# Weight rings of a retention and dilated mixer: four units of hi and lo over two raw slots

## The chip, the core and the metric

The kernel runs on one core of a Trainium2 chip. The metric is the device time of one launch in microseconds (us): the median of several runs. A profiled execution gives the trace, with a span from the first to the last instruction.

## What is computed

Two decoder layers over 512 tokens of width 1024. Each layer adds half of a SwiGLU network, then a token mixer, then half of another SwiGLU network, each on the RMS-normed input. The mixer of layer 0, which the change is about, is

```
h = rms_norm(x, norm_g);  proj = h @ w_in          # 1024 -> 3584
rq, rk, rv, rg, dq, dk, dv = split(proj)           # 8 heads of 64 each
ret = group_norm(retention(rotary(rq), rotary(rk), rv)) * silu(rg)
dil = dilated_attention(rotary(dq), rotary(dk), dv)
out = concat([ret, dil]) @ w_out
```

Layer 1 has a stick-breaking attention in its place. Inputs, weights and output are float32.

## The kernel before

**Two parts of every number.** A float32 operand is cut into `hi` (rounded to the type float32r that TensorE multiplies) and `lo`, the rest; `mm3` gives three matmuls for one product: hi by hi, hi by lo, lo by hi.

**Units.** Weights come in units of 128 x 1024 float32 (512 KB); one unit is a projection of 128 output columns (24 matmuls of 512 columns in `proj_steps`), or half of four heads' values. For every unit a raw copy is loaded by SP's queue into a slot of the role `wraw`, and hi and lo go into two slots of the role `whl`. `give` says which slots a role goes around, and `B` takes the next; a slot is free again when its last reader is done. Ten slots are for weights: before the change four are raw and six hold hi and lo, so three units of hi and lo.

**Two ways to make lo.** `weight` (`split`) casts hi on ScalarE (ACT) and subtracts on VectorE (DVE). In the mixer `weight_dma` is used for g, rq, rk, rv, dq, dk and dv (27 units go this way, since the first of the four gate units goes by `weight`): ACT casts hi, ACT writes minus hi into lo, and GpSimd (POOL) issues a DMA that adds the float32 weight from memory to what lies in lo. DVE has no part in it.

**Order of the mixer.** Four gate units are projected into PSUM banks of the tag `acc` (three of them), the norm's factor `r` comes from one matmul after the first, and `token_r` transposes it on TensorE. Then `stream` goes over the units: rq and rk of the first head pair, the two units of rv for four heads (`values`, two passes of 8 steps, of six matmuls of 256 columns each; both units are read in both passes), rq and rk of the next pair, and so on. `flow.run(n)` runs n steps of it; between them stand the attention's own matmuls: scores (`begin`), and `attend`. On TensorE (PE) this order is fixed by `ordered`. After a projection, DVE turns it (`rot_steps`) with a table that is loaded for each pair (`rot_q`, `rot_k`, 512 KB each), and `pack_q` and `pack_k` move the parts of q (tile `sp`) and of k (tile `ah`) into their places (`qk`, `qlo`) by small DMAs on SP's queue; the scores wait for these. DMA waits stand in SP's queue in order too.

**Output projections.** `out_ffn` computes eight tiles of 128 output columns from 22 chunks in three pieces (8, 7 and 7 chunks, a unit each). Between the pieces units of layer 1's mixer are split ahead (`cut_ahead`): loaded, split, and hi and lo stored to memory. The first four entries of the list are instead the units of rv, which `centre` prepares and stores (`centred`). The last argument of `out_ffn` says how many entries of the list are done there; over tiles 0 to 6 they are spread as evenly as whole numbers allow, tile 7 has none.

Of the kernel before, what the change touches and what calls it, by code (L numbers as in the profile page):

```python
# [18 lines left out]
ALU = mybir.AluOpType  # L19
# [16 lines left out]
def trunk(ctx: ExitStack, tc: tile.TileContext, a: dict, out: bass.AP):  # L36
# [20 lines left out]
    def oldest(role):  # L57

        n = turn_of[role] % len(roles[role])
        return roles[role][n:] + roles[role][:n]  # L60
# [31 lines left out]
    def f32(ap):  # L92
        return ap.bitcast(F32)
# [94 lines left out]

    BY_DMA = ["hyb_" + n for n in ("g", "rq", "rk", "rv", "dq", "dk", "dv")]

    def weight_dma(src, cols):
        raw = B((P, 1024), F32, "wraw")
        hi, lo = (B((P, 1024), F32R, "whl")[:, :cols] for _ in range(2))
        nc.sync.dma_start(raw[:, :cols], src)
        nc.scalar.copy(out=hi, in_=raw[:, :cols])
        nc.scalar.mul(out=lo, in_=f32(hi), mul=-1.0)
        nc.gpsimd.dma_start(lo, src, accum_op=ALU.add)
        return hi, lo

    turns = [0]  # L200
# [85 lines left out]
    def norm_r(ss, epsr=None):  # L286
        while pending:
            norm_sum(*pending.pop(0))
        ps = PS("po")
        mm(ps, ones_ms, ss, start=True, stop=True)  # L290
        r = rstd(ps, NORM_EPS, eps_n, "r")
        if epsr is not None:
            nc.vector.tensor_scalar(out=epsr, in0=ps, scalar1=NORM_EPS, scalar2=GN_EPS, op0=ALU.add, op1=ALU.mult)
        return r
# [288 lines left out]
    def mixer_roles():  # L583
        o = others()
        give(qk=o[:4], v=o[4:8], sp=o[8:11], ah=o[11:14], misc=o[14:15], qlo=o[15:17])
        give(**{f"o{i}": o[17 + i:18 + i] for i in range(8)})
        qlo[:] = [B((P, 2, SEQ), F32R, "qlo") for _ in range(2)]
        for l in qlo:
            nc.gpsimd.memset(f32(l[H1, :, :]), 0.0)
# [241 lines left out]
    def hybrid(ss, gcol_next):  # L831
        order["on"] = True
        mixer_roles()
        gates, held = [], []
        for p in range(4):
            held.append(ACC())
            if p == 0:
                w = weight(a["hyb_g"][0], D)
                proj_tile(None, held[-1], w)
            else:  # L840
                proj_tile(("hyb_g", p), held[-1])
            if p == 0:
                epsr = hpool.tile([P, SEQ], F32, tag="ss", name=nm("epsr"))
                r = norm_r(ss, epsr)
                continue
            if p == 1:
                rtm = token_r(r)
                rtm2 = cpool.tile([P, NB], F32, tag="rtm2", name="rtm2")
                nc.vector.tensor_mul(out=rtm2, in0=rtm, in1=rtm)
                act_set(SILU)  # L850
            for ps in held:
                g = T()
                nc.vector.tensor_mul(out=g, in0=ps, in1=r)
                if len(gates) % 2 == 0:
                    gg = B((P, 2, SEQ), F32, f"o{6 + len(gates) // 2}")
                gates.append(gg[:, len(gates) % 2, :])
                func(gates[-1], g, AF.Silu)
            held = []
        bd = const("bd", P)
        act_set(LNEXP)  # L860
        rot_d = table(a["rot_dil"], "misc")
        for i in range(2):
            nc.gpsimd.tensor_tensor(out=rot_d[:, i, :], in0=rot_d[:, i, :], in1=r, op=ALU.mult)
        outs, vs = [], [[] for _ in range(4)]
        q, k = [], []

        def qk(i):
            if i < 4:
                yield from rot_steps(("hyb_rq", i), table(a["rot_q"][i], "o4"), sw_r, lambda y: pack_q(y, "sp"), q)
                yield from rot_steps(("hyb_rk", i), table(a["rot_k"][i], "o5"), sw_r, lambda y: pack_k(y, "ah"), k)  # L870
            else:
                yield from rot_steps(("hyb_dq", i - 4), rot_d, sw_d, lambda y: pack_q(y, "sp", -0.125), q)
                yield from rot_steps(("hyb_dk", i - 4), rot_d, sw_d, lambda y: pack_k(y, "ah"), k)

        def stream():
            yield from qk(0)
            yield from values(("hyb_rv", 0), rtm2, vs[0])
            for i in range(1, 8):
                yield from qk(i)
                if i in (2, 4, 6):  # L880
                    yield from values(("hyb_rv" if i == 2 else "hyb_dv", (i // 2) % 2), rtm2 if i == 2 else rtm, vs[i // 2])
            yield from out_first("hyb_oa", outs)

        flow = Flow(stream())
        flow.run(26)
        dmask = None
        ready, o = {}, None

        def begin(h):

            nonlocal dmask
            p, e = h // 2, h % 2
            flow.until(k, p + 1)
            if h < 8:
                with tc.high_priority(offset=2 * SOON):
                    ready[h] = ret_scores(e, q[p], k[p], ("ah", "sp")[h % 2])
            else:
                if h == 8:
                    dmask = T(tag="r2")
                    nc.sync.dma_start(dmask, a["dmask"])  # L900
                with tc.high_priority(offset=2 * SOON):
                    ready[h] = dil_scores(e, q[p], k[p], dmask)

        begin(0)
        flow.run(27)
        for h in range(16):
            p, e = h // 2, h % 2
            if h >= 8:
                with tc.high_priority(offset=2 * SOON):
                    ready[h] = dil_turn(e, ready[h], ("ah", "sp")[h % 2])  # L910
                flow.run(2)
            if h < 15:
                begin(h + 1)
            flow.run(5)
            flow.until(vs[p // 2], NB)
            if e == 0:
                o = T(tag="oo")
            attend(vs[p // 2], p, e, ready.pop(h), o)
            if e == 0:
                flow.run(7 if h < 8 else 5)  # L920
            elif h < 8:
                ret_norm(p, o, gates[p], bd, epsr, outs, flow, 6)
            else:
                out_pair(o, outs)
                flow.run(4)
        for _ in flow.steps:
            pass
        ss = out_second("hyb_ob", outs, gcol_next)
        order["on"] = False
        return ss  # L930
# [162 lines left out]
    ahead = [lambda k=("hyb_rv", g, u): centre(k) for g in range(2) for u in range(2)]  # L1093
    ahead += [lambda u=u: cut_ahead(*u) for u in sb]
    us = ffn_seven(sums, a["wd0"], a["wq0"], 0, first)
    ss = out_ffn(a["f1_out"][0], us, 8, ahead, 16)
    ss = hybrid(ss, 16)
    us = ffn_seven(lambda: norm_r(ss), a["wd1"], a["wq1"], 16)
    ss = out_ffn(a["f2_out"][0], us, 24, ahead, 12)
    us = ffn_seven(lambda: norm_r(ss), a["wd2"], a["wq2"], 24)  # L1100
    ss = out_ffn(a["f1_out"][1], us, 32, ahead, 12)
    ss = stick(ss, 40)
    us = ffn_seven(lambda: norm_r(ss), a["wd3"], a["wq3"], 40)
    out_last(a["f2_out"][1], us, 48)
# [126 lines left out]
```

## Time and profile before

| | |
|---|---|
| median of 3 runs | 1932.62 us (1932.16 to 1934.15) |
| the profiled execution's own time | 1934.09 us |
| its span | 1932.4 us |
| PE busy | 1910.3 us (99%) |
| ACT, DVE, POOL busy | 1059.0, 1304.9, 165.8 us |
| mean granted TensorE clock | 0.997 |
| moved by DMA | 341 MB, 176 GB/s over the span |

Busy time of PE is that of overlapping matmuls, whose ends are modelled. The stages that matter here lie, in us from the span's start, at about 270 to 357 (first output projection), 357 to 391 (gates and first rq, rk), 391 to 413 (first values and first scores), 413 to 605 (the rest of the mixer), 605 to 620 (second output projection of the mixer).

### The profile page before, as it was taken

What the parts mean: (1) busy time and instruction counts of PE and PEld (TensorE: products, weight loads), DVE (VectorE), ACT (ScalarE), POOL (GpSimd) and SP (SyncE); (2) the same over time, 40 slices, a digit from 0 to 9 for tenths busy, and PEclk for the clock granted to TensorE, in tenths of its full rate; (3) what the DMA queues carried; (4) which work ended last, traced back from release to release, by engine and by line L of the source; (5) the groups of instructions that cost most, each with busy time, mean ns of one, the idle gap of its engine ahead of it and who ended that gap; (6) DMA issues with size and microseconds to landing.
All of it is one profiled execution on the core that took longest, in us unless ns stands there. A gap on an engine that the chain in (4) does not pass through costs nothing.

```text
span 1932.4 us, 29858 instructions
## 1 busy us (share of the span) xinstructions
PE 1910.3 (99%) x11648; PEld 1716.8 (89%) x11648; DVE 1304.9 (68%) x1854; ACT 1059.0 (55%) x1506; POOL 165.8 (9%) x285
## 2 busy tenths in 40 slices
PE   9999999989999999999999999999999999999998
PEld 7999988778888899998889999888888888999887
DVE  8767855346777877674477677443888878777534
ACT  6466734545776456663344567332666644666423
POOL 0011000112100001100000110000222200111000
PEclk9999999999999999999999999999999999999999
DMA  6386689889852457767734775667555443767433
GB/s 228 101 202 167 140 277 338 249 225 237 178 131 84 140 140 180 167 192 254 276 131 110 197 170 148 208 225 232 161 185 152 137 137 104 201 164 163 117 92 121
DMA packets 107837, 341.00 MB, mean 176 GB/s; under 512 B 13232, under 2 KB 14896, under 8 KB 107696
## 3 DMA queue, kind: packets, MB, share of 16 engines
q1 hardware_dynamic: 90992, 278.54, 44.0%
q0 software_dynamic: 16560, 60.30, 18.0%
q8 instruction: 91, 1.49, 0.3%
q14 instruction: 50, 0.41, 0.1%
q10 hardware_dynamic: 144, 0.26, 0.0%
HBM read 280.33 MB, written 37.75 MB: 165 GB/s over the span
## 4 chain that ended last, share of the span: by engine, by line
PE 94%; DMA 3%; DVE 2%; issue 1%; ACT 1%; SPq 0%; POOL 0%; DVEq 0%; ACTq 0%; POOLq 0%
PE acc L126 46%; PE att L126 45%; PE po L126 2%; DVE whl L225 1%; DMA whl<-centred 1%; PE att L129 0%; DMA cut_sb_k<-whl 0%; DMA qk<-ah 0%; DMA qk<-sp 0%; DVE h L256 0%; DMA cut_sb_v<-whl 0%; DMA wraw<-f_out 0%; ACT whl L224 0%; DMA x<-xT 0%; DMA cut_sb_q<-whl 0%
## 5 line engine op out<-in xcount | busy, mean ns | idle before, releaser
L224 ACT CAST whl<-wraw 128x1024 fp32r<-128x1024 f32 (+4 forms) x308 | 302.8, 989 | 459.0 <-PE acc L126 199.9
L225 DVE TENSOR_TENSOR whl<-wraw,whl 128x1024 fp32r<-128x1024 f32 (+4 forms) x308 | 352.2, 1147 | 259.2 <-ACT whl L224 232.2
L126 PE MATMUL acc<-u,whl 128*128 128x512 f32 (+1 forms) x2244 | 483.5, 377 | 2.1 <-DVE whl L225 2.1
L126 PEld LDWEIGHTS acc<-u,whl 128*128 128x128 f32 x2244 | 403.3, 188 | 80.8 <-DVE whl L225 3.7
L126 PE MATMUL att<-fT,whl 128*128 128x256 f32 x3072 | 379.1, 283 | 0.0
L126 PEld LDWEIGHTS att<-fT,whl 128*128 128x128 f32 x3072 | 373.5, 192 | 0.3
L126 PE MATMUL acc<-h,whl 128*128 128x512 f32 x1248 | 302.1, 394 | 0.9 <-DVE whl L225 0.6
L126 PE MATMUL att<-fB,whl 128*128 128x256 f32 x2304 | 287.2, 283 | 0.0
L126 PEld LDWEIGHTS att<-fB,whl 128*128 128x128 f32 x2304 | 281.2, 192 | 0.2 <-DMA whl<-wq 0.2
L126 PEld LDWEIGHTS acc<-h,whl 128*128 128x128 f32 x1248 | 232.8, 188 | 53.1 <-issue 2.9
L452 POOL DMA_DIRECT2D whl<-wq x88 | 76.4, 868 | 1022.4 <-ACT whl L451 763.0
L450 ACT CAST whl<-wraw 128x1024 fp32r<-128x1024 f32 x88 | 92.4, 1050 | 83.8 <-PE att L126 83.8
L126 PE MATMUL att<-h,whl 128*128 128x512 f32 x576 | 135.8, 389 | 0.0
L126 PEld LDWEIGHTS att<-h,whl 128*128 128x128 f32 x576 | 108.4, 188 | 22.6
L451 ACT ACTIVATE whl<-whl 128x1024 fp32r<-128x1024 f32 x88 | 93.3, 1060 | 2.7
L225 DVE TENSOR_TENSOR whl<-p,whl 128x1024 fp32r<-128x1024 f32 x32 | 39.2, 1224 | 69.5 <-ACT whl L224 69.5
L126 PE MATMUL acc<-whl,h 128*128 128x256 f32 x576 | 75.9, 287 | 4.3 <-DMA whl<-centred 4.3
L126 PEld LDWEIGHTS acc<-whl,h 128*128 128x128 f32 x576 | 73.4, 194 | 5.8 <-DMA whl<-centred 4.7
L323 DVE SCALAR_TENSOR_TENSOR x<-acc,x 128x512 f32<-128x512 f32 (+1 forms) x34 | 22.4, 658 | 69.5 <-PE acc L126 69.4
L225 DVE TENSOR_TENSOR u<-uq,u 128x512 fp32r<-128x512 f32 x88 | 58.9, 688 | 13.4 <-ACT u L224 12.8
L936 POOL TENSOR_SCALAR_AFFINE_SELECT t<-t 128x128 f32<-128x128 f32 x128 | 46.2, 383 | 190.0 <-DVE t L953 124.4
L224 ACT CAST u<-uq 128x512 fp32r<-128x512 f32 x88 | 52.6, 617 | 17.3 <-PE att L126 10.3
(184 smaller groups left out, 2171.8 us busy)
## 6 DMA issues: line engine op xcount, KB each, us to landing
wraw<-wq SPq DMA_DIRECT2D x128, 512.0 KB, 5.0
whl<-wq POOLq DMA_DIRECT2D x88, 512.0 KB, 6.9
wraw<-f_out SPq DMA_DIRECT2D x68, 448.0 KB, 4.3
wraw<-wd SPq DMA_DIRECT2D x46, 512.0 KB, 3.7
wraw<-f_out SPq DMA_DIRECT2D x34, 512.0 KB, 4.7
cut_sb_q<-whl SPq DMA_DIRECT2D x16, 512.0 KB, 3.8
cut_sb_k<-whl SPq DMA_DIRECT2D x16, 512.0 KB, 3.5
cut_sb_v<-whl SPq DMA_DIRECT2D x16, 512.0 KB, 4.8
```

The lines of the kernel that those rows point to most:

```text
L126: return ordered(nc.tensor.matmul(*args, **kw))
L224: nc.scalar.copy(out=hi, in_=src)
L225: nc.vector.tensor_tensor(out=lo, in0=src, in1=f32(hi), op=ALU.subtract)
L323: nc.vector.scalar_tensor_tensor(out=x[d][:, sl], in0=ps[:, sl], scalar=0.5, in1=x[d][:, sl], op0=ALU.mult, op1=ALU.add)
L450: nc.scalar.copy(out=hi, in_=raw)
L451: nc.scalar.mul(out=lo, in_=f32(hi), mul=-1.0)
L452: nc.gpsimd.dma_start(lo, src, accum_op=ALU.add)
L936: nc.gpsimd.affine_select(out=t[:, at:at + P], in_=t[:, at:at + P], pattern=[[1, P]], compare_op=ALU.is_gt, fill=0.0, base=0, channel_mult ...
```

## The change

In the mixer of layer 0 the ten weight slots are dealt out anew: two raw slots and four units of hi and lo, and back to four and three before the last part of its output projection. In `weight_dma` minus hi is taken from the raw unit (rounded as it is written) and comes in the program ahead of hi, with its DMA. The first gate products come after the third gate projection instead of the second, `token_r` with them. The first scores come six steps of the stream later. Of the 40 entries split ahead, 14, 13 and 13 are done in the three output projections in place of 16, 12 and 12.

```diff
+    def minus_hi(lo, src, raw):
+
+        nc.scalar.mul(out=lo, in_=raw, mul=-1.0)
+        nc.gpsimd.dma_start(lo, src, accum_op=ALU.add)
+
     def weight_dma(src, cols):
         raw = B((P, 1024), F32, "wraw")
         hi, lo = (B((P, 1024), F32R, "whl")[:, :cols] for _ in range(2))
         nc.sync.dma_start(raw[:, :cols], src)
+        minus_hi(lo, src, raw[:, :cols])
         nc.scalar.copy(out=hi, in_=raw[:, :cols])
-        nc.scalar.mul(out=lo, in_=f32(hi), mul=-1.0)
-        nc.gpsimd.dma_start(lo, src, accum_op=ALU.add)
         return hi, lo
...
         mixer_roles()
+        raws, ring = oldest("wraw"), oldest("whl")
+        give(wraw=raws[2:], whl=ring + raws[:2])
         gates, held = [], []
         for p in range(4):
...
                 r = norm_r(ss, epsr)
+            if p < 2:
                 continue
-            if p == 1:
+            if p == 2:
                 rtm = token_r(r)
...
         flow = Flow(stream())
-        flow.run(26)
+        flow.run(32)
...
         begin(0)
-        flow.run(27)
+        flow.run(21)
...
         for _ in flow.steps:
             pass
+        raws, ring = oldest("wraw"), oldest("whl")
+        give(wraw=raws + ring[:2], whl=ring[2:])
         ss = out_second("hyb_ob", outs, gcol_next)
...
-    ss = out_ffn(a["f1_out"][0], us, 8, ahead, 16)
+    ss = out_ffn(a["f1_out"][0], us, 8, ahead, 14)
...
-    ss = out_ffn(a["f2_out"][0], us, 24, ahead, 12)
+    ss = out_ffn(a["f2_out"][0], us, 24, ahead, 13)
...
-    ss = out_ffn(a["f1_out"][1], us, 32, ahead, 12)
+    ss = out_ffn(a["f1_out"][1], us, 32, ahead, 13)
```

The order of instructions is set by a scheduler from the program's order and its own estimates, so three places of it are shown. The last number of a name only tells tiles apart.

First, TensorE around the first scores (`att` tiles from `qk` and `qlo`; `acc` from `whl` and `h` are the second pass of the first values). Before, they come after the second of its eight steps:

```order
L126 MATMUL acc_3811<-whl_3745,h_2804 128x256 x2
L126 MATMUL acc_3811<-whl_3746,h_2804 128x256
L126 MATMUL acc_3811<-whl_3745,h_2804 128x256
L126 MATMUL att_3824<-qk_3688,qk_3738 128x384
L126 MATMUL att_3824<-qlo_3458,qk_3738 128x384
```

In the changed kernel, after the eighth:

```order
L126 MATMUL acc_3793<-whl_3758,h_3437 128x256 x2
L126 MATMUL acc_3793<-whl_3759,h_3437 128x256
L126 MATMUL acc_3793<-whl_3758,h_3437 128x256
L126 MATMUL att_3842<-qk_3670,qk_3720 128x384
L126 MATMUL att_3842<-qlo_3440,qk_3720 128x384
```

Nothing else moves on TensorE here: the six steps that stood behind the scores now stand ahead of them.

Second, SP's queue around the moves of the first q and k, which these scores wait for (`sp` is q's, `ah` is k's; `o<-rot_q` and `o<-rot_k` are the tables of the second pair, `wraw` the raw units). Before:

```order
L194 DMA wraw_3990<-hyb_rq 128x1024
L194 DMA wraw_4064<-hyb_rk 128x1024
L734 DMA o_576_3889<-rot_q 128x1024
L654 DMA qk_3688<-sp_3685 64x512 x2
L654 DMA qlo_3458<-sp_3685 64x512
L654 DMA qk_3688<-sp_3685 64x512 x2
L654 DMA qlo_3458<-sp_3685 64x512
L734 DMA o_585_3939<-rot_k 128x1024
L654 DMA qk_3738<-ah_3735 64x512 x4
L194 DMA wraw_4123<-centred_0_2767 128x1024
```

In the changed kernel:

```order
L199 DMA wraw_3972<-hyb_rq 128x1024
L658 DMA qk_3670<-sp_3667 64x512 x2
L658 DMA qlo_3440<-sp_3667 64x512
L658 DMA qk_3670<-sp_3667 64x512 x2
L658 DMA qlo_3440<-sp_3667 64x512
L738 DMA o_570_3871<-rot_q 128x1024
L658 DMA qk_3720<-ah_3717 64x512 x4
L738 DMA o_579_3921<-rot_k 128x1024
L199 DMA wraw_4046<-hyb_rk 128x1024
L199 DMA wraw_4105<-centred_0_2767 128x1024
```

One table moved from ahead of q's moves to behind them, the other, with a raw unit, from ahead of k's moves to behind them.

Third, ACT ahead of the first values (before, `whl_3745` and `whl_3746` are hi and minus hi of rv's first unit, `whl_3776` and `whl_3777` of its second; `o` are the gates). Before:

```order
L195 CAST whl_3745<-wraw_3744 128x1024
L108 ACTIVATE o_535_3601<-t_3635 128x512
L102 ACT_TABLE_LOAD
L196 ACTIVATE whl_3746<-whl_3745 128x1024
L195 CAST whl_3776<-wraw_3775 128x1024
L196 ACTIVATE whl_3777<-whl_3776 128x1024
```

In the changed kernel (`whl_3727` and `whl_3728` are the first unit's, `whl_3758` and `whl_3759` the second's):

```order
L201 CAST whl_3727<-wraw_3726 128x1024
L193 ACTIVATE whl_3728<-wraw_3726 128x1024
L108 ACTIVATE o_529_3583<-t_3581 128x512
L201 CAST whl_3758<-wraw_3757 128x1024
L193 ACTIVATE whl_3759<-wraw_3757 128x1024
L108 ACTIVATE o_529_3583<-t_3617 128x512
L102 ACT_TABLE_LOAD
```

Both units of rv now stand ahead of the last gate and the table load, a unit earlier than before. The scheduler still puts hi first in these two.

## Rows read from the trace of the kernel before

**Rows 1.** The page's part 1, busy time of each engine: us, share of the span, instructions.

```profile
PE 1910.3 (99%) x11648; PEld 1716.8 (89%) x11648; DVE 1304.9 (68%) x1854; ACT 1059.0 (55%) x1506; POOL 165.8 (9%) x285
```

**Rows 2.** The waits of PE over the whole span: who waited for whom, us in total, times, longest.

```profile
PE acc L126 <- DMA whl<-centred: 4.3, 2, 3.2
PE att L126 <- DMA qk<-ah: 3.0, 1, 3.0
PE acc L126 <- DVE whl L225: 2.7, 3, 1.5
```

**Rows 3.** The timeline of PE from the end of the first output projection on: start, us, instructions, and in brackets the idle time before with what ended it.

```profile
342.71 14.84 PE L126 MATMUL acc<-u,whl 128*128 128x512 f32 x64 [1.46 <-DVE whl L225]
...
369.53 22.02 PE L126 MATMUL acc<-h,whl 128*128 128x512 f32 x96
391.39 3.15 PE L126 MATMUL acc<-whl,h 128*128 128x256 f32 x25
397.71 4.46 PE L126 MATMUL acc<-whl,h 128*128 128x256 f32 x35 [3.16 <-DMA whl<-centred]
405.21 0.42 PE L126 MATMUL att<-qk,qk 128*128 128x384 f32 x1 [3.05 <-DMA qk<-ah]
...
406.84 5.70 PE L126 MATMUL acc<-whl,h 128*128 128x256 f32 x36
...
426.80 0.33 PE L126 MATMUL att<-qk,qk 128*128 128x384 f32 x1
...
428.08 3.57 PE L126 MATMUL acc<-h,whl 128*128 128x512 f32 x15
...
442.40 1.58 PE L126 MATMUL acc<-whl,h 128*128 128x256 f32 x11 [1.11 <-DMA whl<-centred]
...
445.04 4.53 PE L126 MATMUL acc<-whl,h 128*128 128x256 f32 x36
```

**Rows 4.** Stretches of time: length, busy us of PE, PEld, DVE, ACT and POOL with their instructions, granted clock, busy share of the DMA engines, GB/s.

```profile
370.00:375.00 5.00, 5.00 (x24) 4.13 (x23) 1.50 (x3) 2.20 (x4) 2.41 (x3) 1.00 0.67 155
375.00:380.00 5.00, 5.00 (x24) 4.14 (x23) 0.69 (x1) 2.53 (x3) 0.87 (x1) 1.00 0.89 205
380.00:385.00 5.00, 5.00 (x23) 4.14 (x23) 0.69 (x1) 3.93 (x4) 0.20 (x1) 1.00 0.80 196
385.00:390.00 5.00, 5.00 (x23) 4.14 (x23) 3.10 (x6) 2.75 (x3) 1.52 (x2) 1.00 0.78 140
395.00:400.00 5.00, 2.29 (x19) 2.29 (x20) 0.63 (x1) 0.00 (x0) 0.00 (x0) 1.00 1.07 256
400.00:405.00 5.00, 2.17 (x19) 1.96 (x17) 0.97 (x2) 0.95 (x2) 0.00 (x0) 1.00 1.04 295
405.00:410.00 5.00, 4.79 (x25) 4.62 (x26) 1.72 (x3) 1.81 (x4) 1.48 (x4) 0.66 0.13 40
407.00:408.00 1.00, 1.00 (x7) 1.00 (x6) 0.96 (x3) 0.59 (x1) 0.60 (x2) 0.50 0.00 0
```

**Rows 5.** The timeline of POOL: the DMAs that add the weight to the second unit of rv, of the first and of the second four heads' values.

```profile
388.56 0.86 POOL L197 DMA_DIRECT2D whl<-centred  x1 [2.90 <-ACT whl L196]
...
432.61 0.88 POOL L197 DMA_DIRECT2D whl<-centred  x1 [2.22 <-ACT whl L196]
```

**Rows 6.** The timeline of ACT ahead of the first values. L195 is hi, L196 minus hi; the first pair is that of rv's first unit, the second that of its second.

```profile
380.49 1.05 ACT L195 CAST whl<-wraw 128x1024 fp32r<-128x1024 f32 x1 [2.91 <-PE acc L126]
381.45 0.62 ACT L108 ACTIVATE o<-t 128x512 f32<-128x512 f32 x1
382.09 1.28 ACT L102 ACT_TABLE_LOAD   x1
383.38 1.06 ACT L196 ACTIVATE whl<-whl 128x1024 fp32r<-128x1024 f32 x1
385.93 1.05 ACT L195 CAST whl<-wraw 128x1024 fp32r<-128x1024 f32 x1 [1.48 <-PE acc L126]
387.01 1.06 ACT L196 ACTIVATE whl<-whl 128x1024 fp32r<-128x1024 f32 x1
```

**Rows 7.** DMA issues of single stretches, with the size and the us from issue to landing, in this order: a raw unit of rv at 360 to 380, rv's first unit at 383 to 388, its second at 388 to 389, a table and the later second unit at 432 to 434.

```profile
wraw<-centred SPq DMA_DIRECT2D x1, 512.0 KB, 5.1
whl<-centred POOLq DMA_DIRECT2D x1, 512.0 KB, 5.4
whl<-centred POOLq DMA_DIRECT2D x1, 512.0 KB, 9.1
o<-rot_q SPq DMA_DIRECT2D x1, 512.0 KB, 11.6
whl<-centred POOLq DMA_DIRECT2D x1, 512.0 KB, 9.7
```

**Rows 8.** The chain of work that ended last, in order of time: start, us, what.

```profile
396.14 8.25 DMA qk<-ah
```

**Rows 9.** The timeline of ACT, and then of PE, at the end of the second output projection, whose tile 6 has two entries split ahead.

```profile
956.32 1.79 ACT L224 CAST whl<-wraw 128x896 fp32r<-128x896 f32 x2 [6.19 <-DMA cut_sb_k<-whl]
...
960.58 9.36 PE L126 MATMUL acc<-u,whl 128*128 128x512 f32 x40 [0.65 <-DVE whl L225]
```

**Rows 10.** The timeline of ACT (the logarithm of the norm's factor) and of DVE (the first two gate products).

```profile
364.85 0.67 ACT L108 ACTIVATE t<-po,eps_n 128x512 f32<-128x512 f32 x1
...
368.86 1.29 DVE L853 TENSOR_TENSOR t<-acc,r 128x512 f32<-128x512 f32 x2
```

## The prediction

> **What bounds the kernel now.** I read the page's busy times first, then the waits of PE, then PE's timeline where these waits fall, and last who was late. PE is busy in 1910.3 of 1932.4 us [rows 1]: only what shortens PE's idle time or its slow time can pay. Its waits in and just ahead of the changed stage are four: 3.16 and 1.11 us for the DMA that adds the weight to the second unit of rv, 3.05 for the moves of the first k, 1.46 for a DVE subtraction at the end of the first output projection [rows 2, 3]. Waits of 3.16 and 3.05 us follow within ten, and then the clock falls: 0.66 over 405 to 410, and 0.50 (1.2 of 2.4 GHz) in 407 to 408, while PE is busy [rows 4]. The price is read from equal work: 36 matmuls of the values took 5.70 us there and 4.53 at full clock, so 1.17; the eight score matmuls took 406.84 - 405.21 = 1.63 there and 428.08 - 426.80 = 1.28 later, so 0.35. With that the stage loses 1.46 + 3.16 + 3.05 + 1.52 + 1.11 = 10.3 us, and no more than this can come back.
>
> **The second unit of rv (3.16).** Both units of rv are read in both passes, so with three units in the ring the second unit can be cut only when the first rq is done: its hi begins at 385.93, its minus hi at 387.01 [rows 6], its DMA is issued at 388.56 [rows 5], takes 9.1 us [rows 7] and PE goes on at 397.71. With a fourth unit it takes the place that the last gate unit leaves at 380.49, one projection earlier. There the new order on ACT puts the pair of this unit ahead of the last gate and of the table load (1.28), which before stood inside the first unit's pair [rows 6]: hi 1.05, minus hi 1.06, done at 382.6, and with the 0.5 from there to the issue that POOL took before (388.07 to 388.56) the DMA goes out at 383.1. At the slow 9.1 us it lands at 392.2, at the 5.4 of the unit before it [rows 7] at 388.5. PE wants it after 24 matmuls, at 391.39 + 3.15 = 394.5 [rows 3]. So 2.3 us to spare: **gain 3.16**; bounds 3.16 and, if the unit is cut no earlier than before, 0.
>
> Two raw slots must not eat this. The raw load of that unit may go out when the unit two before it, the first rk, is cut: which on ACT stands behind the first two gates. With the second gate product at 372.2 (worked out under what costs nothing), its gate at 0.62 and minus hi at 1.06 [rows 6] that is 373.9, and 5.1 us for the load [rows 7] gives 379.0, 1.5 ahead of 380.49.
>
> **The first scores (3.05).** They come six steps, 36 matmuls, later: 4.53 us [rows 3]. PE reached them at 397.71 + 4.46 = 402.17; without the wait above at 399.0, and six steps later at 403.5. The moves of k landed so that PE went on at 405.21, so at an unchanged landing 1.7 us of waiting is left. What makes them land earlier is SP's queue: one table of 512 KB goes from ahead of k's moves to behind them, the other from ahead of q's to behind, and at the 256 to 295 GB/s of these stretches [rows 4] 512 KB are 1.8 to 2.0 us. That would take off the 1.7; since the moves took 8.25 us [rows 8] on full DMA engines I leave 0.5. **Gain 2.55**, bounds 1.35 (moves land as before) and 3.05.
>
> The Trainium skill, "DMA: Bandwidth & Descriptors", section "Issuing engines are not separate DMA queues", speaks against this: DMAs of all issuing engines run on the same 16 DMA engines and interleave. By it a unit that is fetched earlier on POOL's queue takes from k's moves what the table gave them, and this term would be its lower bound of 1.35; the row of full engines (1.07 and 1.04 at 395 to 405) agrees, the idle room ahead of them does not.
>
> **The clock (1.52).** The later wait of 1.11 alone is followed by 36 matmuls at 4.53 us [rows 3], so a single short wait does not bring the clock down. With 0.5 left of the two: **gain 1.5**, bounds 0 and 1.5.
>
> **The later second unit (1.11).** Its DMA went out at 432.61 [rows 5] and took 9.7 [rows 7]. One unit earlier in the ring is 5.5 us (96 matmuls of four units in 22.02 [rows 3]), and 1.11 are needed. **Gain 1.1**, bounds 0 and 1.1.
>
> **End of the first output projection (1.46).** Tile 6 has three entries before and two now. The second output projection has two there already, and what it shows is another wait: ACT's cast for the last piece stands ahead of that for the second piece and waits until the stores of the last unit split ahead have landed (6.19 us), and PE loses 0.65 [rows 9]. The same order will stand here. **Gain 0.8**, bounds 0 (the stores are slower here, on fuller DMA engines) and 1.46. The two other projections get one entry more each, in tiles that then have one or two like their neighbours: 0, bounds 0 and a loss of 0.65 each, the size of that same wait.
>
> **What costs nothing.** Minus hi from raw instead of hi: the same operation at 1.06. Hi behind minus hi, in the 10 of 27 units where the scheduler did it: hi is 1.05 later, hidden behind a DMA of at least 5.4 [rows 7]. The gates: all three `acc` banks are held, so the fourth gate projection can begin only after the first product, which needs r. On ACT the pair of the first rq now stands ahead of the logarithm (364.85 [rows 10]) and waits for its raw load. That load goes out when the third gate unit is cut, 342.71 + 14.84 + 2.1 = 359.7; with 5.1 and the pair the logarithm begins at 366.9, 2.0 late, so the products too: the first is done at 368.86 + 0.65 + 2.0 = 371.5. The fourth projection begins one projection after 369.53 [rows 3], at 375.0: hidden with 3.5 to spare. The values and q wait for nothing of this, since `token_r` now stands where r is surely there. Giving the slots back at the end: the next loads wait for projections that are two units gone.
>
> **New waits.** Moves of later head pairs share full DMA engines with the units fetched earlier. I take 0.65, a wait as a late unit makes it in [rows 9]; bounds 0 and 3.9 (worked out below).
>
> **Sum.** 3.16 + 2.55 + 1.5 + 1.1 + 0.8 - 0.65 = 8.5 us. The profiled execution took 1934.09, 1.7 more than its span, and would take 1925.6. It is 1.5 above the median of the runs; from the median of 1932.62 the forecast is **1924.2**.
>
> **Rivals.**
> *A, the waits come back in part.* PE would want everything behind 413 earlier by 3.16 + 3.05 + 1.5 = 7.7 us, so the DMA engines must have done as much earlier. Idle room before: 4.3 us in 370 to 390 (shares 0.67, 0.89, 0.80, 0.78) and 4.4 in 405 to 410 (0.13) [rows 4], together 8.7. If only the first is used, 3.4 return: gain 5.1, **1927.5**.
> *B, they return whole, only elsewhere*: the units fetched earlier lie on the same full DMA engines as the moves of the next head pairs, which are late in place of the first. Then only the clock (the waits are spread) and the output projection stay: 1.5 + 0.8, less 0.65 of new waits, **1931.0**. For it: engines at 1.07 and 1.04 in 395 to 405; against it: the room. The page's rule on shared DMA engines leads here if there is no room at all.
> *C, slower: two raw slots.* A raw load waits until the unit two back is cut, so two units take a load and a pair at least. PE goes through the six units between 412.5 and 449.6 (406.84 + 5.70 and 445.04 + 4.53) in 6.2 us each. At the slowest load here, 11.6 [rows 7], the ring gives one in (11.6 + 2.1) / 2 = 6.85: 0.65 x 6 = 3.9 lost, gain 4.6. It decides where the six units lose 12.4, the gain of 8.5 and 3.9 more, so 2.1 each: at 8.3 a unit, a load of 14.5: **1936.5**. Against it: that is 2.9 above the longest load, and two others in [rows 7] took 5.1 and 5.4.
> *D, minus hi first does nothing*: so in 17 of 27 units; it changes no number above.
>
> **How the numbers follow.** Forecast 0.68 (1921.8 to 1927; all upper bounds give 1922.3), A 0.11, B 0.14, C 0.07. A measurement of this kernel tells 0.2% (3.9 us) from no change. Faster are the forecast and A, 0.79; the same is B, 0.14; slower C, 0.07. The range goes from the upper bounds less 0.7 to B: 1921.6 to 1931.0; it leaves out C and the half of B above it.
>
> **What would show it.** Right: no wait of PE for `centred` above 0.5 us, at most 1 us before the first scores, clock 1.00 throughout 400 to 415, a DVE wait of about 0.65 at the end of the first output projection, and DMA engines that no longer stand idle after the first scores. Wrong: PE waits for `qk` at a later pair (B), ACT casts of raw units that wait for SP's loads (C), or a first gate product that comes after the third gate projection.

## The result and the profile after

The changed kernel is slower: 1938.37 us (median of nine runs, 1935.03 to 1943.69), beside 1932.16 for the kernel before in the same nine rounds; 1.003 times as long, 95% interval 1.0021 to 1.004. The forecast was 1924.2. The profiled execution took 1937.97 at a span of 1936.3, 3.9 more span than before, so its rows account for the larger part of the 6.2.

Part 1 of the page of after, as in [rows 1]:

```profile
PE 1913.1 (99%) x11648; PEld 1718.7 (89%) x11648; DVE 1304.5 (67%) x1854; ACT 1057.2 (55%) x1506; POOL 166.2 (9%) x285
```

PE does the same work in 2.8 us more, and idles 1.1 more. The waits of PE of after over the whole span, as in [rows 2]: both waits for `centred` are gone, two new ones stand in their place, for an ACT result at L784 (the square in the first retention norm) and for a gate unit (`hyb_g`), and the wait for k's moves is still there.

```profile
PE att L126 <- ACT t L784: 3.5, 1, 3.5
PE acc L126 <- DVE whl L229: 3.5, 4, 1.5
PE att L126 <- DMA qk<-ah: 2.6, 1, 2.6
PE acc L126 <- DMA whl<-hyb_g: 1.5, 1, 1.5
```

The timeline of PE of after, for [rows 3]:

```profile
317.14 15.27 PE L126 MATMUL acc<-u,whl 128*128 128x512 f32 x66 [1.24 <-DVE whl L229]
332.62 24.33 PE L126 MATMUL acc<-u,whl 128*128 128x512 f32 x106 [0.21 <-DVE whl L229]
356.79 5.80 PE L126 MATMUL acc<-h,whl 128*128 128x512 f32 x24
...
365.58 10.74 PE L126 MATMUL acc<-h,whl 128*128 128x512 f32 x46 [1.54 <-DMA whl<-hyb_g]
...
392.99 11.67 PE L126 MATMUL acc<-whl,h 128*128 128x256 f32 x96
407.29 0.66 PE L126 MATMUL att<-qk,qk 128*128 128x384 f32 x1 [2.63 <-DMA qk<-ah]
...
409.77 16.15 PE L126 MATMUL acc<-h,whl 128*128 128x512 f32 x63
...
442.62 4.52 PE L126 MATMUL acc<-whl,h 128*128 128x256 f32 x36
450.69 1.88 PE L126 MATMUL att<-t,bd 128*128 128x512 f32 x2 [3.55 <-ACT t L784]
```

The values (96 matmuls from 392.99) now run through without a stop, as forecast. What is lost stands before and behind them. Stretches of after, with the columns of [rows 4]:

```profile
410.00:411.00 1.00, 1.00 (x3) 0.76 (x3) 0.64 (x2) 0.96 (x2) 0.99 (x3) 0.50 1.02 270
410.00:415.00 5.00, 5.00 (x16) 3.94 (x16) 1.34 (x3) 2.96 (x4) 2.14 (x5) 0.66 0.54 158
451.00:452.00 1.00, 1.00 (x3) 0.33 (x2) 0.48 (x1) 0.45 (x1) 0.00 (x0) 0.50 1.11 270
450.00:455.00 5.00, 4.31 (x14) 3.13 (x15) 1.85 (x4) 4.16 (x8) 0.89 (x1) 0.66 0.95 254
```

The granted clock falls twice, to 0.50 (1.2 of 2.4 GHz) behind the wait of 2.63 and again behind that of 3.55.

**The ledger of the two traces**, after less before, in us. After begins the first gate matmul 0.6 sooner. From there: the gate unit +1.54; rv's second unit -3.16; the wait before the first scores 2.63 for 3.05, -0.42; the slow clock there, +1.24 (the eight scores took 2.48 for 1.63 before, the 63 matmuls behind them 16.15 for 14.59, and the 1.17 that 36 matmuls of the values lost before is gone); rv's later second unit -1.11; the retention norm +3.55; slow clock behind it +1.7 (ten matmuls and the gap between them, 3.86 for 2.14). With the 0.6 that is +2.7; the `po` matmuls behind them begin 3.0 later in the trace. A wait in the second output projection adds 0.83 (1.48 for 0.65), and 3.9 is the difference of the spans.

**Who was late.** ACT's waits from 357 to 460 us, first of the kernel before, then of after (columns as in [rows 2]):

```profile
ACT whl L195 <- PE acc L126: 24.8, 11, 2.9
```

```profile
ACT whl L193 <- DMA wraw<-hyb_rk: 6.1, 2, 4.1
ACT whl L201 <- DMA wraw<-hyb_rq: 5.0, 2, 3.5
ACT whl L201 <- DMA wraw<-hyb_g: 3.0, 1, 3.0
```

Before, ACT never waits here for a raw load: its casts wait until PE gives a place of hi and lo free. After, it waits 18.8 us in all for raw loads, and what stands behind the waiting cast is late too. The timelines of SP's queue, DVE and ACT show it for the 3.55:

```profile
426.41 2.54 SPq L738 DMA_DIRECT2D o<-rot_q  x1
434.86 0.69 DVE L731 TENSOR_TENSOR tp<-acc,o 128x512 f32<-128x512 f32 x1 [4.82 <-DMA o<-rot_q]
441.34 0.59 SPq L199 DMA_DIRECT2D wraw<-hyb_rk  x1
446.65 1.06 ACT L193 ACTIVATE whl<-wraw 128x1024 fp32r<-128x1024 f32 x1 [4.09 <-DMA wraw<-hyb_rk]
448.67 0.58 ACT L703 COPY t<-po 64x512 f32<-64x512 f32 x1
449.28 0.69 DVE L704 TENSOR_TENSOR oo<-po,t 64x512 f32<-64x512 f32 x1 [5.04 <-ACT t L703]
450.01 0.63 ACT L784 ACTIVATE t<-oo 128x512 f32<-128x512 f32 x1 [0.76 <-DVE oo L704]
```

A table of the third pair is issued late, DVE waits for it, so q's moves go out late; the raw load of the last rk stands behind them in SP's queue and is issued at 441.34. ACT waits for it. Behind this unit's two casts in ACT's order stands the copy of a retention output (L703), which has nothing to do with that unit; DVE's sum (L704) needs the copy, and the norm's square needs the sum. With the ring undone (below) the table is as late: q of that pair is written at 434.99, after a wait of 7.43, here at 436.96 after 5.85. But there the last rk was loaded at 415.42, no cast waits for it, and the copy comes at 441.37.

### The profile page after: what moved, and what is told of

It reads as the page before. It is cut to its first block, busy times and chain, and to the rows that moved or that the text cites. A ratio compares the mean times of both kernels' runs of the same rounds, so it can differ in the third digit from the quotient of the medians.

```text
span 1936.3 us, 29852 instructions
## 1 busy us (share of the span) xinstructions
PE 1913.1 (99%) x11648; PEld 1718.7 (89%) x11648; DVE 1304.5 (67%) x1854; ACT 1057.2 (55%) x1506; POOL 166.2 (9%) x285
## 4 chain that ended last, share of the span: by engine, by line
PE 89%; DMA 6%; DVE 2%; ACT 1%; issue 1%; SPq 1%; POOL 0%; DVEq 0%; ACTq 0%; POOLq 0%
PE att L126 45%; PE acc L126 41%; PE po L126 2%; DMA wraw<-hyb_rq 1%; DVE whl L229 1%; DMA cut_sb_v<-whl 1%; DMA wraw<-f_out 1%; DMA cut_sb_q<-whl 1%; DMA qk<-ah 0%; PE att L129 0%; ACT whl L228 0%; DMA o<-rot_q 0%; DMA wraw<-hyb_g 0%; SPq L658 0%; DVE h L260 0%
## 5 line engine op out<-in xcount | busy, mean ns | idle before, releaser
L228 ACT CAST whl<-wraw 128x1024 fp32r<-128x1024 f32 (+3 forms) x308 | 302.7, 989 | 469.6 <-PE acc L126 195.4
L229 DVE TENSOR_TENSOR whl<-wraw,whl 128x1024 fp32r<-128x1024 f32 (+3 forms) x308 | 351.7, 1147 | 266.5 <-ACT whl L228 224.2
L228 ACT CAST u<-uq 128x512 fp32r<-128x512 f32 x88 | 52.7, 617 | 17.2 <-PE att L126 10.3
```

Of the source, the lines that this page charges most:

```text
L228: nc.scalar.copy(out=hi, in_=src)
L229: nc.vector.tensor_tensor(out=lo, in0=src, in1=f32(hi), op=ALU.subtract)
```

## Experiments

The theory: with two raw slots the loads go out late, ACT waits for them in order and holds up what PE needs. Rival 1: the loss comes from the other edits (later gates, later scores, 14/13/13). Rival 2: four units, fetched earlier, take the DMA engines from the moves and from each other, whatever the number of raw slots.

All diffs are against the changed kernel; every row has its own rounds beside the kernel before (1931.86 to 1932.68). The last column is the sum of ACT's waits for `wraw` from 357 to 460 us in the profiled execution.

| | raw, units (gates / to the fourth head / behind) | us | ratio to before, 95% | ACT for raw loads |
|---|---|---|---|---|
| kernel before | 4,3 | 1932.16 | | 0 |
| changed kernel | 2,4 | 1938.37 | 1.0021 to 1.004 | 18.8 |
| ring_undone | 4,3 | 1929.65 | 0.9977 to 0.9994 | 0 |
| two_raw_three_units | 2,3 | 1933.72 | 1.0003 to 1.002 | 11.1 |
| oldest_as_raw | 2,4, other two raw | 1933.87 | 0.9997 to 1.0015 | 12.5 |
| four_raw_four_units | 4,4 / 4,4 / 2,4 | 1933.46 | 0.9997 to 1.0015 | 0 |
| four_four_then_three | 4,4 / 4,4 / 4,3 | 1932.62 | 0.9991 to 1.0009 | 0 |
| fourth_unit_late | 4,3 / 4,4 / 4,3 | 1926.62 | 0.9965 to 0.9984 | 3.6 |
| fourth_late_then_two | 4,3 / 4,4 / 2,4 | 1930.14 | 0.998 to 1.0003 | 4.2 |
| redeal_after_gates | 4,3 / 2,4 / 2,4 | 1940.57 | 1.0028 to 1.0052 | 32.8 |
| redeal_after_gates_oldest | 4,3 / 2,4 / 2,4, other two raw | 1942.98 | 1.0039 to 1.0066 | 31.1 |

**The ring undone.**

```diff
-        raws, ring = oldest("wraw"), oldest("whl")
-        give(wraw=raws[2:], whl=ring + raws[:2])
...
-        raws, ring = oldest("wraw"), oldest("whl")
-        give(wraw=raws + ring[:2], whl=ring[2:])
```

> The changed kernel with the old dealing of the ten slots (four raw, three units of hi and lo); minus hi ahead of hi, the later gates, the later scores and 14/13/13 stay. Theory (two raw slots make raw loads late, ACT stands in order before them and holds up what PE needs): the waits of 1.54 us (first rq) and 3.55 us (square of the first retention norm) go, and so does the slow clock after 450; the waits for the second unit of rv (3.16 and 1.11) come back, less some because nothing else is lost; 1932 to 1934 us. Rival 1 (the loss comes from the later gates, the later scores or 14/13/13): it stays at 1936 to 1939. Rival 2 (four units overload the DMA engines): 1932 to 1934 too; the run with four raw slots and four units tells it from the theory.

1929.65, a little better than expected: the deal of the slots alone costs 8.7 us, the rest of the change is worth 2.2, and rival 1 falls. The timeline of PE has rv's two waits back, and no wait before the first scores or the norm:

```profile
396.72 10.07 PE L126 MATMUL acc<-whl,h 128*128 128x256 f32 x71 [2.77 <-DMA whl<-centred]
...
438.52 1.58 PE L126 MATMUL acc<-whl,h 128*128 128x256 f32 x11 [0.71 <-DMA whl<-centred]
```

**Two raw slots and three units.** Two slots lie idle in the mixer; at its end all four are raw again.

```diff
-        give(wraw=raws[2:], whl=ring + raws[:2])
+        give(wraw=raws[2:], whl=ring)
...
-        raws, ring = oldest("wraw"), oldest("whl")
-        give(wraw=raws + ring[:2], whl=ring[2:])
+        give(wraw=raws[:2] + oldest("wraw"), whl=oldest("whl"))
```

> Two raw slots and three units: two of the ten slots lie idle in the mixer; all other edits as in the changed kernel. With the changed kernel (two raw, four units: 1938.4), the ring undone (four, three: 1929.7) and four and four (1933.5) this fills the square. Theory (raw slots): with two raw slots nothing is loaded ahead while the DMA engines have room at 340 to 355 us, and the bytes come due where they are full; share of the DMA engines there about 0.5 as in the changed kernel, and 1934 to 1938 us, 4 or more above the ring undone. Rival 2 (the fourth unit overloads them): 1930 to 1931.

1933.72, 4.1 above the ring undone: fewer raw slots cost this without any fourth unit, so rival 2 cannot be the whole. It is not refuted either: of the 8.7 the other 4.6 come only with the fourth unit. The room that the expectation names is seen in the stretch 340 to 355 us, of the ring undone, of this kernel and of the changed one in this order:

```profile
340.00:355.00 15.00, 15.00 (x68) 12.43 (x67) 6.67 (x8) 6.21 (x7) 2.73 (x3) 1.00 0.86 297
```

```profile
340.00:355.00 15.00, 15.00 (x67) 12.40 (x67) 7.68 (x8) 7.38 (x9) 1.84 (x2) 1.00 0.68 235
```

```profile
340.00:355.00 15.00, 15.00 (x68) 12.42 (x67) 6.97 (x8) 5.78 (x8) 1.84 (x2) 1.00 0.49 177
```

With four raw slots the DMA engines are filled to 0.86 here, with two to 0.68 and 0.49, since there is no place to load into. The share of this kernel is 0.68, not the 0.5 that was expected. The wait for the norm's square is here too, again behind a raw load (2.9 us of ACT's waiting, for a rq), by the timeline of PE:

```profile
450.07 1.13 PE L126 MATMUL att<-t,bd 128*128 128x512 f32 x2 [2.25 <-ACT t L784]
```

It stands in five of the six kernels here that have two raw slots up to the fourth head (2.2 to 4.2 us), and in none with four.

**Four raw slots and four units.** Two slots of attention outputs that are free until then make up for the two that are taken.

```diff
-        raws, ring = oldest("wraw"), oldest("whl")
-        give(wraw=raws[2:], whl=ring + raws[:2])
+        extra = roles["o2"] + roles["o3"]
+        give(wraw=oldest("wraw"), whl=oldest("whl") + extra)
...
+            if h == 4:
+                raws = oldest("wraw")
+                give(wraw=raws[2:], whl=[i for i in oldest("whl") if i not in extra] + raws[:2])
```

> The changed kernel with four raw slots and four units up to the fourth head: the two slots that lack are those of the third and fourth attention output, which are free until then; after it two raw slots and four units as in the change. Theory (number of raw slots): raw loads go out two units earlier, no cast of ACT waits for a raw load by more than 1 us in 360 to 460, the waits of 1.54 and 3.55 us go and the clock stays up after 450; the wait for the second unit of rv stays away; 1929 to 1933 us. Rival 2 (the units fetched earlier overload the DMA engines): the moves of the first k and the DMAs of minus hi take longer still, the waits stay or grow, 1937 us or more.

1933.46, neither: ACT no longer waits for raw loads and the norm's wait is gone, but a gate unit is waited for, and the first scores wait 1.71 for k's moves. The chain, and the timeline of PE:

```profile
355.20 0.81 issue
356.01 0.01 POOLq L194
356.03 10.26 DMA whl<-hyb_g
```

```profile
366.33 10.74 PE L126 MATMUL acc<-h,whl 128*128 128x512 f32 x46 [2.39 <-DMA whl<-hyb_g]
```

The order on POOL names the cause. `whl_3503` is the second gate unit's, `whl_3535` the third's, `whl_3588` the fourth's:

```
L194 DMA whl_3588<-hyb_g 128x1024
L194 DMA whl_3503<-hyb_g 128x1024
L194 DMA whl_3535<-hyb_g 128x1024
```

With the ring undone they go out as 3503, 3535, 3588. The fourth unit's place is free first, so the scheduler cuts the gate that PE needs last ahead of the one that it needs next: that one's DMA is issued 1.0 us ahead of the first gate matmul (356.0) instead of 2.4 (354.1), and takes 10.3 instead of 9.1 us. The Trainium skill, "DMA: Bandwidth & Descriptors", section "Issuing engines are not separate DMA queues", says that DMAs share the engines whoever issues them; no run here shows that the longer landing is that, since with the fourth unit late (below), where the gates keep their order, the same DMA takes 10.3 us too. The profiled execution took 1929.07, 4.4 below its median, so the rows hold the kind of loss and not all of it.

**The fourth unit late.** Three units in the gates, the fourth place from the first rq of the stream on.

```diff
-        raws, ring = oldest("wraw"), oldest("whl")
-        give(wraw=raws[2:], whl=ring + raws[:2])
...
+        extra = roles["o2"] + roles["o3"]
+        give(wraw=oldest("wraw"), whl=oldest("whl") + extra)
         bd = const("bd", P)
...
+            if h == 4:
+                give(wraw=oldest("wraw"), whl=[i for i in oldest("whl") if i not in extra])
...
-        raws, ring = oldest("wraw"), oldest("whl")
-        give(wraw=raws + ring[:2], whl=ring[2:])
```

> Four raw slots throughout, three units of hi and lo in the gates, and a fourth only from the first rq of the stream up to the fourth head, in the two slots of the third and fourth attention output; three again after it. All other edits as in the changed kernel. Theory: the gates run as with the ring undone (no wait for a gate unit), the two waits for the second unit of rv (2.77 and 0.71 us there) go, and the wait before the first scores is at most 2 us: 1926 to 1929 us, 1 to 3 below the ring undone (1929.65). Rival 2 (a unit that is fetched earlier only takes the DMA engines from the moves): the waits come back as waits for moves of q and k, 1929 to 1933.

1926.62, 0.9975 of before, the lowest median here. The timeline of PE: the two waits for the second units of rv are gone, the first scores and the norm come without a wait, and three other waits are left, for a gate unit, for rk and for moves:

```profile
364.09 10.75 PE L126 MATMUL acc<-h,whl 128*128 128x512 f32 x46 [1.01 <-DMA whl<-hyb_g]
...
388.34 5.32 PE L126 MATMUL acc<-h,whl 128*128 128x512 f32 x22 [1.36 <-DMA whl<-hyb_rk]
393.50 11.68 PE L126 MATMUL acc<-whl,h 128*128 128x256 f32 x96
405.02 0.34 PE L126 MATMUL att<-qk,qk 128*128 128x384 f32 x1
...
433.23 0.41 PE L126 MATMUL att<-qk,qk 128*128 128x384 f32 x1 [1.71 <-DMA qk<-ah]
...
443.83 1.13 PE L126 MATMUL att<-t,bd 128*128 128x512 f32 x2
```

The wait for rk is the swap of the gates once more: POOL issues the DMA of rv's second unit at 374.66, ahead of that of rk at 377.01, which takes 11.3 us. The expectation that no gate unit would be waited for missed. By the medians the late fourth unit is worth 3.0 us against the ring undone, and 2.4 and 2.3 in the two pairs below that each take one more edit back. This trace can't show where the 3.0 come from: its execution took 1930.25, the slowest of the nine, beside 1930.52 for the profiled one of the ring undone.

**Which half.** These exchange the deal behind the fourth head (`if h == 4` of the one in the other).

> Four raw slots and four units from the first gate unit to the fourth head, and four and three behind it. Against four_raw_four_units (1933.46; two and four behind the fourth head) only the second half differs, against fourth_unit_late (1926.62) only the gates. Theory: the fourth unit in the gates is what costs, because the DMAs that add the weight to the second and third gate unit go out together and PE waits 2.4 us for the first: 1931 to 1934 us. Rival: two raw slots behind the fourth head cost it: 1926 to 1928.

> The fourth unit from the end of the gates, and behind the fourth head two raw slots and four units in place of four and three. Theory: behind the fourth head there are no retention tables to be loaded after the fourth pair, the DMA engines have room, and the number of raw slots is worth nothing: 1926 to 1928 us. Rival (raw slots cost everywhere): 1930 to 1934.

1932.62 and 1930.14. The first is as slow as with two and four behind, so what separates it from fourth_unit_late, 6.0 us, comes from the fourth unit in the gates; in its trace PE waits 3.43 for the same gate unit. Against the ring undone a fourth unit from the gates on costs 3.0 and 3.8 us even with four raw slots. In the second, two raw slots behind the fourth head seem to cost 3.5, but its runs spread from 1925.3 to 1937.5 and the intervals touch: not settled.

**The other two slots as raw.**

```diff
-        give(wraw=raws[2:], whl=ring + raws[:2])
+        give(wraw=raws[:2], whl=ring + raws[2:])
```

> The changed kernel, but the two raw slots are the two that have been free longest instead of the two used last. Theory: the loads of the first two gate units go out at about 340 and 343 us as before (345.6 and 347.6 in the changed kernel), the bunch of four loads at 354.7 to 356.1 comes apart, and the wait of 1.54 us at the first rq goes, with the hold-up of the norm's logarithm by some us; the wait of 3.55 us at the retention norm stays, since it comes later in the steady rate: 1936 to 1937.5 us. If the bunch is the cause of all that follows, 1933; if it is the cause of nothing, 1938.4.

1933.87, 4.5 below the changed kernel and more than expected: the gate unit's wait goes, with two raw slots still, and PE starts the first scores 4.1 us sooner (403.19 for 407.29), after a wait of 2.02. The wait for the norm's square stays, at 3.54, as expected.

**The change's deal behind the gates**, so that the gates' loads are as with the ring undone; and the same with the other two slots.

```diff
-        raws, ring = oldest("wraw"), oldest("whl")
-        give(wraw=raws[2:], whl=ring + raws[:2])
...
+        raws, ring = oldest("wraw"), oldest("whl")
+        give(wraw=raws[2:], whl=ring + raws[:2])
         bd = const("bd", P)
```

> The change's own deal (two raw slots, four units, no other slots), but made behind the gates instead of ahead of them. Theory: the gates run as with the ring undone (no wait for a gate unit, four raw units loaded ahead), so 1.5 us and more come back of the change's 1938.4; the wait for the square of the first retention norm, behind a raw load that is late with two slots, stays with its slow clock: 1931 to 1934 us. If only the gates' loads matter: 1927, as with the fourth unit from other slots; if the steady stretch is all: 1937.

> As redeal_after_gates (1940.57), but the two raw slots that stay are those that were filled first and are free first, instead of last. Theory of the choice of slots: the raw load of the first rq goes out at about 351 us again (357.3 in redeal_after_gates) and that of the first rk at about 353 (362.8), the two units of rv are loaded before ACT wants them, the wait of 7.1 us before the first scores falls to 2 us or less: 1931 to 1934 us. Theory of the number: two raw slots keep the raw loads of the next pairs behind the moves, ACT waits for them, 1937 us or more.

1940.57 and 1942.98: the theory that the gates' bunch of loads is the larger part missed, the first by 6.6 us from its range, and so did the choice of slots. No gate unit is waited for in the first, but PE waits 7.09 before the first scores. Its chain shows why:

```profile
374.55 7.66 DMA wraw<-centred
...
386.06 1.06 ACT whl L201
...
387.14 5.39 DMA wraw<-hyb_rq
...
392.64 1.06 ACT whl L193
393.69 0.53 ACT sp L652
...
403.27 6.62 DMA qk<-ah
```

Load, cut, next load into the slot just cut, cut, in turn; and behind the last of these cuts, in ACT's order, stands the cast of q itself (`sp`, L652), whose moves and then k's are what PE waits for. The first kernel has the gates of fourth_late_then_two and its deal behind the fourth head; between them it has two raw slots for four, and takes 10.4 us more. So behind the gates the number of raw slots is the cause. In the gates it is not settled: two raw slots went there without a wait for a gate unit (oldest_as_raw), and four with one of 1.01. Nor does the table's last column rank the kernels by itself: with a fourth unit in the gates 3.0 and 3.8 us are lost at a column of 0.

**The scores where they were.**

```diff
-        flow.run(32)
+        flow.run(26)
...
-        flow.run(21)
+        flow.run(27)
```

> The changed kernel with the first scores where they were (26 and 27 steps instead of 32 and 21). The moves of the first k landed at 407.3 us, and PE would come to the scores 4.5 us sooner, so theory: the wait before them grows from 2.63 to about 6 to 7 us, and 1942 us; if the later place is itself what makes the moves or the units of the next pairs late, 1936 us or less.

With the change's deal 1941.80, by this line of PE's timeline as expected:

```profile
408.08 0.66 PE L126 MATMUL att<-qk,qk 128*128 128x384 f32 x1 [7.47 <-DMA qk<-ah]
```

That execution was the slowest of its six, 1947.67.

> The ring undone, and the first scores after 26 steps of the stream as before. With the ring undone PE waits 2.77 us for the second unit of rv and not for the moves of the first k. Theory: with the scores 4.5 us sooner the wait for the moves comes back, 2 to 3 us, and the slow clock (up to 1.5 us): 1931 to 1933 us, that is as before the change; if the later scores are worth nothing, 1929.7.

With the ring undone 1933.87. The later scores are thus worth 4.2 us there, and are the part of the change that pays; with the change's deal it is 3.4, but those intervals (1.003 to 1.0064 and 1.0021 to 1.004) overlap.

**The remaining edits**, each taken back on its own: hi cast ahead of minus hi, the gate products after the second projection, and 16/12/12.

> The ring undone, and hi cast ahead of minus hi again, minus hi made from hi. Theory: worth little, since hi and minus hi take 1.05 us each and the DMA behind minus hi 5 us or more, and the scheduler often put hi first anyway; where minus hi goes 1.05 us later the waits for the second unit of rv (2.77 and 0.71) may grow by 1 us each: 1929.7 to 1931.7 us.

> The ring undone, and the first two gate products after the second gate projection as before. Theory: the later gates give PE nothing that it waited for, and hold the fourth gate projection, which needs a free bank, no longer than it can bear; 1929 to 1930.5 us. If the later place is worth something it is 1931 us or more, if it costs something 1928.5 or less.

> The ring undone, and 16, 12 and 12 units split ahead again. Theory: at the ends of the three output projections PE waited 1.46, 0.65 and 0.6 us in the kernel before and 1.45, 1.5 and 0.6 in the changed one, so nothing is gained: 1929 to 1930 us. If 14/13/13 is worth the 0.8 that the prediction gave it: 1930.5.

> The late fourth unit (1926.6 us) with 16, 12 and 12 units split ahead. Theory: as for the ring undone, no difference or up to 1 us less, since the later output projections have one entry less each: 1925.5 to 1927 us. If 14/13/13 is worth 0.8: 1927.5.

> The late fourth unit (1926.6 us) with the first gate products after the second gate projection. With four units the DMA engines are full from 355 us on and PE waits 1.0 us there for a gate unit; if the logarithm and the products on ACT and DVE come sooner nothing that PE waits for does: 1926 to 1927.5 us. A rival: the transposes of the norm's factor then come a projection sooner than that factor is sure to be there, and PE waits for them, 1928 us or more.

With the ring undone 1931.20, 1929.89 and 1929.63 for its 1929.65; with the late fourth unit 1927.21 (16/12/12) and 1927.62 (gates early) for 1926.62. Gates and counts are worth nothing that shows. Minus hi first may be worth 1.5; the intervals (0.9987 to 1.0005 and 0.9977 to 0.9994) overlap. The single edits don't add up: the ring undone and the scores early leave only these three, and 1933.87 is 1.9 above before; that stays open.

## Why the prediction was wrong, point by point

- **The second unit of rv (3.16) and the later one (1.11): right.** By the timeline of POOL its DMA went out at 385.12, where 383.1 was worked out, and both waits went.

```profile
385.12 0.86 POOL L194 DMA_DIRECT2D whl<-centred  x1 [3.74 <-ACT whl L193]
```

- **"Two raw slots must not eat this": the step that failed.** It followed one raw load, that of this unit, and found it 1.5 us ahead; ACT in fact waited 1.95 for it, which the spare 2.3 bore. The other loads were followed for what PE wants from their own unit only. Not asked was what else stands behind a cast on ACT while it waits: the retention norm's square, q's own cast. Only for the logarithm was that followed (366.9; it came at 371.34, since the load took 8.9 instead of 5.1 us), and there PE waited for nothing, as said. In place of no cost the runs show 4.1 us for two raw slots with three units and 10.4 behind the gates with four. The timeline of ACT in the gates:

```profile
369.43 1.05 ACT L201 CAST whl<-wraw 128x1024 fp32r<-128x1024 f32 x1 [3.46 <-DMA wraw<-hyb_rq]
370.38 1.05 ACT L193 ACTIVATE whl<-wraw 128x1024 fp32r<-128x1024 f32 x1
371.34 0.67 ACT L108 ACTIVATE t<-po,eps_n 128x512 f32<-128x512 f32 x1
```

- **Rival C had the cause and the wrong price.** It put two raw slots as a rate: a load and a pair shared by two units, which decides only from loads of 14.5 us on. The raw load behind which 3.55 us were lost took 4.9; what decided is when it was issued, behind moves in SP's queue and behind the cut of the unit two back, and what stood behind it on ACT. The measured time is on C's side of the forecast and 1.9 beyond its 1936.5, but C alone is about half of it: of the 8.7 us that the deal costs, 4.1 come with two raw slots and three units, and 4.6 only with the fourth unit on top, which the prediction took for a gain. In four_raw_four_units and four_four_then_three the cut that comes too early explains such a loss; in the changed kernel the gate units are cut in order, and which part of its waits is the fourth unit's stays open.
- **The first scores (2.55): 0.42.** Taking tables and a raw unit from ahead of the moves brought these forward by little: the chain of after has them issued 1.25 us later than [rows 8], while PE itself, held by the gate unit, comes to the values 1.6 later (392.99 for 391.39). That 0.35 was more than eaten by the transfer, 9.35 for 8.25 us, on DMA engines at 1.06 from 397 to 406. The lower bound of 1.35 was too high as well, since it held the landing fixed: rival B, for this one transfer. With the ring undone the wait is gone: six steps do pay, in another deal.

```profile
397.39 9.35 DMA qk<-ah
```

- **The clock (1.5): a loss of 3.** The inference from [rows 3], that one short wait leaves the clock up, was drawn from 1.11 us. Behind single waits of 2.63 and 3.55 us the granted clock fell, and 1.24 and 1.7 us more went there. Nor is it the length of the wait alone: behind the 2.39 of four_raw_four_units it stayed at 1.00.
- **The output projection (0.8): 0.** The wait split in two, 1.24 and 0.21, for 1.46. Between kernels with the same 14 entries PE's waits for DVE in this projection ran from nothing to 2.4 us, and going back to 16 changes no time that shows: the wait of [rows 9] was not a rule.
- **New waits (0.65): 5.9** (1.54, 3.55, and 0.83 in the second output projection).
- **The gates at no cost: half right.** The fourth projection was not held, as said. But the first gates' raw loads, which the step did not follow, went out at 345.6 and 347.6 instead of 339.5 and 342.7, since the slots kept were the last used. Four loads of 512 KB (two gate units, two tables) bunched behind them at 354.7 to 356.1, and the second gate's DMA, issued at 355.72, 1.1 us ahead of the first gate matmul where the ring undone has 2.4, took 9.8 us beside them: 1.54.

## What to carry to other kernels

A buffer taken from the loads to deepen the stage behind them is a loan from the engine that cuts in order: price it by listing, for each load that now goes out later, everything that stands behind its cast on that engine, not only the unit's own reader. Give a deeper ring only slots that nobody else fills, and from the point where its wait stands: a place that is free too early lets a scheduler cut first what is needed last, so look at the order of the cuts after each new deal. To tell a wait that went from one that only moved, undo the deal of the slots alone.

## What the runs showed of the hardware

The DMA that adds a 512 KB unit onto minus hi took 9.1 to 11.7 us where it ran beside raw loads and tables on full DMA engines, about twice the 5.4 that [rows 7] have at best. The granted clock fell to 0.50 behind single waits of 2.63 and 3.55 us in the changed kernel, while PE was busy without a stop; behind a single wait of 1.11 us it did not [rows 3], nor behind one of 2.39 us in the gates of four_raw_four_units (1.00 from 366 to 375).
